# A hybrid encoder on one core: two query tiles loaded ahead of the bias rows, and epsilon of the convolution's layer norm added on VectorE

## The chip, the cores and the metric

The kernel runs on one core of a Trainium2 chip. The time is device time in microseconds (us) of a whole execution; a kernel is timed by the median of several executions. Engines are named as in the profile: PE is TensorE's matmuls, PEld its weight loads, DVE is VectorE, ACT ScalarE, POOL GpSimd, and SP (SyncE) issues the transfers (DMAs).

## The reference

One layer of an encoder runs over two requests with shared weights: a prompt of 512 tokens and a sample of 1024 tokens, model width 1024, everything in float32. Cut to what matters:

```python
h = rmsnorm(x); z = h @ w_in                      # q, k, v, and two conv halves ca, cb
a = window_attn(q, k, v, bias, |i-j| <= 128, sink) # 8 heads, 2 kv heads, blocks of 128 queries
c = dwconv31(ca * sigmoid(cb))                     # 512 channels
c = silu(layernorm(c, g, b))                       # (c - mean) * rsqrt(var + 1e-6) over the channels
x = x + concat(a, c) @ w_out
h = rmsnorm(x); u = dwconv3(h @ w_up)
x = x + (silu(u[:FF]) * u[FF:]) @ w_down           # FF = 2816
y = rmsnorm(x)
```

The attention adds to each score a bias that depends on head and distance alone: for each head one table of 128 x 384 numbers serves all blocks.

## The kernel before

Every float32 product is made of three matmuls: each operand is split into a high and a low part, and high x high, high x low and low x high are accumulated. The projection has the lines L354, L355 and L357 for these three, 128 x 128 weights against 512 columns.

The stages overlap. TensorE first does the prompt's input projection (to about 96 us), then the sample's (to about 345 us), into which the prompt's attention, convolution norms and output projection are woven step by step: they are Python generators (`attention`, `scores`, `values`, `conv_norm`, `out_half`) that are advanced between the projection's matmuls. In the same way the sample's attention is woven into the prompt's feed-forward (to about 600 us); the sample's norms and output projection follow, and then its feed-forward up (from about 740 us) and down (from 1148 us), whose matmuls stand in an order written out by hand. In the earlier part a scheduler of the framework orders each engine's instructions, by the order in which the code issues them and by its own simulated times. On-chip buffers come from a pool of numbered slots (q0..., h0..., s0...): a new tile waits until the last users of its slot are done, so the issue order of the tiles also decides which slot each gets. Names such as h56_198 are slot h56, tile number 198.

The places that matter here:

- *Queries.* `evac` with "q" splits a projected query block and writes it to a scratch buffer in DRAM, qsd, in pieces of 128 KB (L448). `load_q(u)` loads it back for one unit u (one block of 128 queries, one kv head, four heads) as a tile of 128 x 512 numbers, 256 KB (L646). `scores(u)` calls `load_q(u)` and `load_q(u + 1)`, multiplies with the keys (L682, two matmuls of 256 to 384 columns per head), and adds the bias on DVE (L689).
- *Bias.* `load_bias` loads eight rows, one for each head, 192 KB each (L631), from a DRAM table bbd. It is called once, after the prompt's projection, and before any `load_q`.
- *Behind the scores.* ACT takes exponentials (L707), DVE completes the sums and takes a reciprocal (L705, L710, L711), ACT and POOL scale (L715, L717), and TensorE transposes the result (L737) for the product with the values.
- *Convolution.* A depthwise convolution of 31 taps runs mostly as DVE operations (L409); some taps are done by ACT and POOL (L401, L402). A finished channel block is written to DRAM, cvd (L419).
- *The convolution's layer norm.* `conv_norm(i)` runs for each of the 12 blocks of 128 tokens: transposes (L812), mean and variance on DVE (L814, L815), then 1/sqrt(var + eps) on POOL as two operations of one number per partition (`rstd_of`, L214: times 1/n plus eps; L215: to the power -1/2), then the normalisation on DVE (L818), transposes back (L824), scale and shift on ACT (L827), tanh and the product with it (L829 to L832).
- *Splitting weights.* `split` casts a raw weight chunk to its high part on ACT (L237) and subtracts on POOL or DVE (L238). ACT also evacuates finished banks of the projection (L430).
- *The prompt's feed-forward.* Its small convolution of three taps runs on DVE (L977) and ACT (L981).

Of the kernel before, what the change touches and what calls it, by code (L numbers as in the profile page):

```python
# [29 lines left out]
EPS = 1e-6  # L30
# [143 lines left out]
def tile_hybrid_encoder(ctx: ExitStack, tc: tile.TileContext, xs, xsT, rel_bias, norm_attn_g, w_in,  # L174
                        attn_sink, w_out, norm_ffn_g, w_up, w_down, norm_final_g, packed, onehot, outs):
    nc = tc.nc
# [18 lines left out]
    def sm(n):  # L195
        return sb.tile([n])

    def bank(job):
        return banks.tile([NT], among=use[job])
# [13 lines left out]
    def rstd_of(ss, n, out):  # L213
        nc.gpsimd.tensor_scalar(out, ss, 1.0 / n, EPS, op0=ALU.mult, op1=ALU.add)  # L214
        nc.gpsimd.tensor_tensor(out, out, nhalf[:], op=ALU.pow)  # L215

    def power(out):
        nc.gpsimd.tensor_tensor(out, out, nhalf[:], op=ALU.pow)
# [122 lines left out]
    def drain(queue):  # L341
        while queue:
            advance(queue)
# [284 lines left out]
    def load_bias():  # L628
        for h in range(NH):
            bt = sb.tile([3 * P])  # L630
            nc.sync.dma_start(bt[:], bass.AP(b0.tensor, b0.offset + h * NT + P - 1, [[NH * NT - 1, P], [1, 3 * P]]))  # L631
            bias.append(bt)

    load_bias()


    blocks = [(G, b) for G in GR for b in range(G["nb"])]
    NB = len(blocks)
    qt, cats, units, rawcat = {}, {}, {}, {}
# [1 line left out]
    def load_q(u):  # L641
        if u < 2 * NB and u not in qt:
            q = sb.tile([GRP, P], F32R)
            i, kv = divmod(u, 2)
            nt, b = divmod(i, 4)
            nc.sync.dma_start(q[:].bitcast(F32), qsd[nt][b, :, kv * GRP:(kv + 1) * GRP, :])  # L646
            qt[u] = q

    def window(i):
        G, b = blocks[i]  # L650
        return [k for k in (b - 1, b, b + 1) if 0 <= k < G["nb"]]
# [13 lines left out]
    def scores(u):  # L665
        i, kv = divmod(u, 2)
        load_q(u)
        if blocks[min(u + 1, 2 * NB - 1) // 2][0] is blocks[i][0]:
            load_q(u + 1)
# [51 lines left out]
    def cat_of(i, part):  # L721
        if (i, part) not in cats:
            cats[i, part] = (sb.tile([4, P], F32R), sb.tile([4, P], F32R))
        return cats[i, part]
# [45 lines left out]
    def split_cat(i, eng):  # L770
        raw = rawcat.pop(i)
        hi, lo = cats[i, 0] = (sb.tile([4, P], F32R), sb.tile([4, P], F32R))
        flat = lambda t: t[:].rearrange("p j t -> p (j t)")
        nc.scalar.copy(flat(hi), raw[:])
        eng.tensor_tensor(flat(lo), raw[:], flat(hi).bitcast(F32), op=ALU.subtract)
# [16 lines left out]
    def load_conv(i):  # L792
        G, b = blocks[i]
        cv = cvs[i] = sb.tile([4, P])
        nc.sync.dma_start(cv[:], cvd[G["g"]][:, :, b * P:(b + 1) * P])
        if G["g"] == 1 and i not in rawcat:
            load_cat(i)

    def conv_norm(i):
        G, b = blocks[i]  # L800
        if G["g"] == 0:
            drain(convs)
        cat = cat_of(i, 1)
        if i not in cvs:
            load_conv(i)
            yield 0.0
        cv = cvs.pop(i)
        if G["g"] == 1:
            split_cat(i, nc.vector)
        pt = bank("norm")  # L810
        for c in range(4):
            nc.tensor.transpose(pt[:, c * P:(c + 1) * P], cv[:, c, :], ident[:])  # L812
        st, mv, rs = sm(6), sm(2), sm(1)
        nc.vector.bn_stats(st[:], pt[:])  # L814
        nc.vector.bn_aggr(mv[:], st[:])  # L815
        rstd_of(mv[:, 1:2], 1.0, rs[:])
        xh = sb.tile([CCH])
        nc.vector.tensor_scalar(xh[:], pt[:], mv[:, 0:1], rs[:], op0=ALU.subtract, op1=ALU.mult)  # L818
        del pt
        for _ in range(YN if G["g"] == 0 else 3):  # L820
            yield 0.0
        p2 = bank("norm")
        for c in range(4):
            nc.tensor.transpose(p2[:, c * P:(c + 1) * P], xh[:, c * P:(c + 1) * P], ident[:])  # L824
        y, t = sb.tile([4, P]), sb.tile([4, P])
        for c in range(4):
            nc.scalar.activation(y[:, c, :], p2[:, c * P:(c + 1) * P], AF.Identity,  # L827
                                 scale=lng[:, c:c + 1], bias=lnb[:, c:c + 1])
        nc.scalar.activation(t[:], y[:], AF.Tanh)  # L829
        nc.vector.scalar_tensor_tensor(t[:], t[:], 1.0, y[:], op0=ALU.add, op1=ALU.mult)  # L830
        nc.scalar.copy(cat[0][:], t[:])
        nc.vector.tensor_tensor(cat[1][:], t[:], cat[0][:].bitcast(F32), op=ALU.subtract)  # L832
        yield 0.0
# [73 lines left out]
    def prompt():  # L907
        yield from attention(0, 8, {u: conv_norm(u - 4) for u in range(4, 8)})
        kt.clear(), vt.clear(), qt.clear(), bias.clear()
        pace.update(rate=RBO, late=CLO)  # L910
        for n in range(2):
            for kc in range(KC):
                if (kc, n) not in wor:
                    load_wo(kc, n)
            yield 0.0
            for kc in range(KC):
                split_wo(kc, n, kc % 2 < DW)
                if kc % 2 == 1:
                    yield 0.0
            for i in range(4):  # L920
                if n == 0 and i == 3:
                    for kc in range(WOP):
                        load_wo(kc, 1)
                yield from out_half(i, n)
            wo.clear()
        yield from make_h2(0, 0)
# [129 lines left out]
    def sample():  # L1056
        sink_columns()
        yield from attention(8, 24)
        kt.clear(), vt.clear(), qt.clear(), bias.clear(), score_rows.clear()
        use.update(norm="a")  # L1060
        pace.update(rate=RN)
        for m in range(KC + WOA):
            if m in (2, 4):
                load_cat(m // 2 + 3)
            if m < KC:
                load_wo(m, 0)
            if m >= WOA:
                split_wo(m - WOA, 0, True)
                yield 0.0
        drain(late)  # L1070
        for m in range(NE):
            yield from conv_norm(4 + m)
        load_conv(4 + NE)
        for kc in range(KC):
            load_wo(kc, 1)
            yield 0.0
# [174 lines left out]
    def right_halves():  # L1251
        for kc in range(KC):
            split_wo(kc, 1, True)
            yield 0.0

    side.extend((right_halves(), conv_norm(4 + NE)))
    side.extend(pair_sums(p) for p in (*range(SOON), NPAIR - 1))
    pace.update(rate=2.2)
# [607 lines left out]
```

## Time and profile before

| | us |
|---|---|
| three runs | 1490.27, 1491.04, 1492.84 |
| median | 1491.04 |
| profiled execution | 1491.56 |
| its span, first to last instruction | 1489.8 |
| mean granted TensorE clock | 0.998 |
| TensorE's longest wait | 2.90 |

The profile's page gives the busy time of each engine; a list of waits gives, for each engine and line, the time it stood idle and what released it; a timeline gives start and duration of each instruction (or of a run of equal ones, "x4"), with the idle time before it and its releaser in brackets. A windows row gives the length of a stretch, then the busy time of PE, PEld, DVE, ACT and POOL with the number of instructions, the granted clock (1.00 is full), the share of the time that the 16 DMA engines were busy, and GB/s. Matmuls are pipelined: the duration of one (0.39 us) is longer than the distance between two starts.

### The profile page before, as it was taken

The numbers are of one execution on the slowest core, as the hardware profiler recorded it, in microseconds if no ns is written. First come the engines' busy times: TensorE is split into PE (matmuls) and PEld (weight loads), VectorE is DVE, ScalarE is ACT, GpSimd is POOL, SyncE is SP. The second block draws the span as 40 slices with busy tenths as digits, with TensorE's granted clock in tenths as the row PEclk, the third lists the DMA queues.
The fourth block names the chain that finished last, engine by engine and source line by source line (L and its number), as shares of the span: only waits on it lengthen the run. The fifth ranks groups of instructions, "written<-read, shape, count | busy, mean of one in ns | idle before, by whom it ended". The sixth has DMA issues, their size and how long they took to land.

```text
span 1489.8 us, 19831 instructions
## 1 busy us (share of the span) xinstructions
PE 1473.5 (99%) x6808; PEld 1221.1 (82%) x6808; DVE 1136.3 (76%) x1619; ACT 796.9 (53%) x1415; POOL 677.7 (45%) x539
## 2 busy tenths in 40 slices
PE   9999999999999999999999999999999999999998
PEld 7878888887888888878888888888888888888886
DVE  5999988778689875666868777777776945569875
ACT  8556565336777776444465544554445633444254
POOL 6962445235665576763326555555544000003345
PEclk9999999999999999999999999999999999999999
DMA  8963346274433337883213333333332672356644
GB/s 290 294 187 85 93 120 188 86 234 133 132 114 119 121 121 226 268 312 131 82 57 107 106 106 107 106 102 100 103 107 83 225 264 86 110 173 228 217 166 170
DMA packets 222049, 225.60 MB, mean 151 GB/s; under 512 B 12363, under 2 KB 162131, under 8 KB 221820
## 3 DMA queue, kind: packets, MB, share of 16 engines
q1 hardware_dynamic: 221804, 224.08, 47.0%
q8 instruction: 53, 0.87, 0.2%
q14 instruction: 48, 0.39, 0.1%
q10 hardware_dynamic: 144, 0.26, 0.0%
HBM read 165.29 MB, written 60.05 MB: 151 GB/s over the span
## 4 chain that ended last, share of the span: by engine, by line
PE 48%; POOL 3%; DMA 3%; issue 2%; DVE 2%; ACT 1%; SPq 0%; POOLq 0%; DVEq 0%; ACTq 0%
PE w L1237 9%; PE w L1239 9%; PE w L1238 9%; PE w L1589 5%; PE w L1588 5%; PE w L1587 5%; PE u L848 1%; PE u L850 1%; PE u L849 1%; DMA h<-in_w_out 1%; POOL q L1097 1%; PE c L850 1%; PE c L849 1%; PE c L848 1%; DMA c<-in_norm_final_g 0%
## 5 line engine op out<-in xcount | busy, mean ns | idle before, releaser
L238 POOL TENSOR_TENSOR q<-q,q 128x1024 fp32r<-128x1024 f32 x71 | 173.1, 2441 | 126.6 <-ACT q L237 49.4
L1100 POOL TENSOR_TENSOR q<-q,q 128x512 fp32r<-128x512 f32 x101 | 141.9, 1412 | 151.8 <-ACT q L1223 140.8
L1100 DVE TENSOR_TENSOR h<-h,h 128x512 fp32r<-128x512 f32 (+2 forms) x202 | 154.9, 800 | 67.8 <-ACT h L1104 30.2
L1589 PE MATMUL w<-h,h 128*128 128x512 f32 x462 | 179.7, 389 | 0.0
L1587 PE MATMUL w<-h,h 128*128 128x512 f32 x458 | 178.2, 389 | 0.0
L1588 PE MATMUL w<-h,h 128*128 128x512 f32 x458 | 178.2, 389 | 0.0
L1237 PE MATMUL w<-h,q 128*128 128x512 f32 x448 | 174.9, 390 | 1.1 <-ACT w L1320 0.8
L1239 PE MATMUL w<-h,q 128*128 128x512 f32 x448 | 174.3, 389 | 0.0
L1238 PE MATMUL w<-h,q 128*128 128x512 f32 x426 | 165.7, 389 | 0.0
L409 DVE SCALAR_TENSOR_TENSOR c<-c,cvw,c 128x512 f32<-128x512 f32 x209 | 156.8, 750 | 3.0
L354 PE MATMUL u<-h,q 128*128 128x512 f32 x368 | 146.7, 399 | 2.0 <-DVE h L977 2.0
L355 PE MATMUL u<-h,q 128*128 128x512 f32 x368 | 144.4, 392 | 0.0
L357 PE MATMUL u<-h,q 128*128 128x512 f32 x360 | 141.3, 393 | 0.1
L1097 POOL TENSOR_TENSOR q<-q,q 128x1024 f32<-128x1024 f32 x12 | 32.8, 2748 | 230.4 <-DMA h<-gb 190.0
L1104 ACT CAST h<-h 128x512 fp32r<-128x512 f32 x120 | 71.8, 620 | 96.4 <-DVE h L1100 43.9
L354 PE MATMUL b<-h,q 128*128 128x512 f32 x264 | 105.5, 400 | 0.0
L357 PE MATMUL b<-h,q 128*128 128x512 f32 x264 | 104.4, 395 | 0.0
L355 PE MATMUL b<-h,q 128*128 128x512 f32 x264 | 103.9, 394 | 0.0
L1589 PEld LDWEIGHTS w<-h,h 128*128 128x128 f32 x462 | 86.7, 188 | 17.8
L1588 PEld LDWEIGHTS w<-h,h 128*128 128x128 f32 x458 | 86.0, 188 | 18.0
L1587 PEld LDWEIGHTS w<-h,h 128*128 128x128 f32 x458 | 86.0, 188 | 17.8
L1237 PEld LDWEIGHTS w<-h,q 128*128 128x128 f32 x448 | 84.1, 188 | 19.1 <-ACT w L1320 1.3
(447 smaller groups left out, 3620.5 us busy)
## 6 DMA issues: line engine op xcount, KB each, us to landing
q<-in_w_up SPq DMA_DIRECT2D x88, 512.0 KB, 4.4
ga<-q SPq DMA_DIRECT2D x64, 256.0 KB, 2.0
h<-ga SPq DMA_DIRECT2D x57, 256.0 KB, 3.3
q<-in_w_in SPq DMA_DIRECT2D x28, 512.0 KB, 5.3
h<-in_w_down SPq DMA_DIRECT2D x52, 256.0 KB, 3.6
q<-in_x_sample SPq DMA_DIRECT2D x15, 512.0 KB, 7.0
h<-qsd SPq DMA_DIRECT2D x24, 256.0 KB, 2.9
x1d<-q SPq DMA_DIRECT2D x11, 512.0 KB, 4.4
```

Of the source, the lines that this page charges most:

```text
L238: ins = (nc.vector if dve else nc.gpsimd).tensor_tensor(lo[:], raw[:], hi[:].bitcast(F32), op=ALU.subtract)
L354: nc.tensor.matmul(out, whi[:, kc, :], hi[:], start=(kc == 0), stop=False)
L355: nc.tensor.matmul(out, whi[:, kc, :], lo[:], start=False, stop=False)
L357: nc.tensor.matmul(out, wlo[:, kc, :], hi[:], start=False, stop=(kc == KC - 1))
L409: nc.vector.scalar_tensor_tensor(acc[:], src(t), w(t), acc[:], op0=ALU.mult, op1=ALU.add)
L1100: (eng or nc.vector).tensor_tensor(out, a, b, op=ALU.subtract)
L1237: nc.tensor.matmul(out, whi[:, s], hi[:], start=(start and c == 0), stop=False, **go)
L1238: nc.tensor.matmul(out, whi[:, s], lo[:], start=False, stop=False, **go)
L1239: nc.tensor.matmul(out, wlo[:, s], hi[:], start=False, stop=(stop and c == 3), **go)
L1587: nc.tensor.matmul(out, sh[:, c], th[:], start=(p == 0), stop=False)
L1588: nc.tensor.matmul(out, sh[:, c], tl[:], start=False, stop=False)
L1589: nc.tensor.matmul(out, sl[:, c], th[:], start=False, stop=(p == NPAIR - 1))
```

## The change

```diff
@@ -631,9 +631,6 @@
             nc.sync.dma_start(bt[:], bass.AP(b0.tensor, b0.offset + h * NT + P - 1, [[NH * NT - 1, P], [1, 3 * P]]))
             bias.append(bt)
 
-    load_bias()
-
-
     blocks = [(G, b) for G in GR for b in range(G["nb"])]
     NB = len(blocks)
     qt, cats, units, rawcat = {}, {}, {}, {}
@@ -645,6 +642,10 @@
             nt, b = divmod(i, 4)
             nc.sync.dma_start(q[:].bitcast(F32), qsd[nt][b, :, kv * GRP:(kv + 1) * GRP, :])
             qt[u] = q
+
+    load_q(0)
+    load_q(1)
+    load_bias()
 
     def window(i):
         G, b = blocks[i]
@@ -813,7 +814,8 @@
         st, mv, rs = sm(6), sm(2), sm(1)
         nc.vector.bn_stats(st[:], pt[:])
         nc.vector.bn_aggr(mv[:], st[:])
-        rstd_of(mv[:, 1:2], 1.0, rs[:])
+        nc.vector.tensor_scalar_add(rs[:], mv[:, 1:2], EPS)
+        power(rs[:])
         xh = sb.tile([CCH])
         nc.vector.tensor_scalar(xh[:], pt[:], mv[:, 0:1], rs[:], op0=ALU.subtract, op1=ALU.mult)
         del pt
```

The query tiles of units 0 and 1 are now issued in the code ahead of the eight bias rows, and take their slots ahead of them. In the layer norm eps is added by a DVE operation, and POOL does the power alone (`power`, L218). Later lines move by one to three: L646 becomes L643, L682 L683, L707 L708, L715 L716, L737 L738, L818 L820, L830 L832, L832 L834, L977 L979. The scheduler's order changes with it at many places; three of them follow.

SP, the end of the prompt's projection: the last bias rows (bbd) and the first query tiles (qsd), up to the write of a convolution block (cvd). Before:

```order
L631 DMA q6_202_1153<-bbd_406 128x384
L631 DMA h3_200_1148<-bbd_406 128x384
L631 DMA q6_202_1153<-bbd_406 128x384
L631 DMA q3_201_1150<-bbd_406 128x384 x2
L631 DMA q1_203_1156<-bbd_406 128x384
L646 DMA h26_205_1187<-qsd0_163 128x512
L646 DMA h32_206_1189<-qsd0_163 128x512
L231 DMA q10_225_1324<-in_w_in 128x8x128
L646 DMA h11_231_1369<-qsd0_163 128x512
L419 DMA cvd0_169<-h56_125_721 128x512
```

Now:

```order
L631 DMA q6_202_1152<-bbd_406 128x384
L643 DMA h3_200_1148<-qsd0_163 128x512
L631 DMA q6_202_1152<-bbd_406 128x384
L643 DMA q3_201_1150<-qsd0_163 128x512
L631 DMA q1_203_1155<-bbd_406 128x384
L631 DMA h26_205_1161<-bbd_406 128x384
L631 DMA h32_206_1163<-bbd_406 128x384
L643 DMA q3_201_1150<-qsd0_163 128x512
L231 DMA q10_225_1324<-in_w_in 128x8x128
L643 DMA h11_231_1369<-qsd0_163 128x512
L419 DMA cvd0_169<-h56_125_721 128x512
```

Unit 0's tile moved from the sixth bias row's rear (slot h26) to the place of a bias row (slot h3), unit 1's (slot h32 before, q3 now) follows two rows later, and two bias rows went behind. The cvd write kept its place behind the burst. On PE the first scores moved two matmuls forward in the last bank of the projection.

ACT, the same time: the tap of the convolution into slot h56 (L401), the exponentials of unit 0, and the weight cast L237. Before:

```order
L401 ACTIVATE h56_198_1126<-q11_114_671,cvw_308 128x512
L707 ACTIVATE q4_204_1159,s26_208_1192<-q4_204_1159,s25_207_1191 128x256
L707 ACTIVATE h55_209_1200,s26_208_1192<-h55_209_1200,s25_207_1191 128x256
L707 ACTIVATE q13_210_1212,s26_208_1192<-q13_210_1212,s25_207_1191 128x256
L430 ACTIVATE q9_212_1237<-b1_41_1173 128x512
L707 ACTIVATE q13_210_1212,s26_208_1192<-q13_210_1212,s25_207_1191 128x256
L709 ACTIVATE s27_211_1218<-s27_211_1218 128x4
L707 ACTIVATE q9_212_1237,s29_215_1242<-q9_212_1237,s28_214_1241 128x256
L715 ACTIVATE q4_204_1159<-q4_204_1159,s26_208_1192 128x256
```

Now:

```order
L401 ACTIVATE h56_198_1126<-q11_114_671,cvw_308 128x512
L237 CAST q12_244_1456<-q10_225_1324 128x1024
L708 ACTIVATE h55_209_1196,s26_208_1192<-h55_209_1196,s25_207_1191 128x256
L708 ACTIVATE q13_210_1201,s26_208_1192<-q13_210_1201,s25_207_1191 128x256 x2
L430 ACTIVATE q9_211_1217<-b1_41_1177 128x512
L708 ACTIVATE q9_211_1217,s26_208_1192<-q9_211_1217,s25_207_1191 128x256
L710 ACTIVATE s27_212_1219<-s27_212_1219 128x4
L708 ACTIVATE h56_215_1245,s29_214_1241<-h56_215_1245,s28_213_1240 128x256
L708 ACTIVATE h42_216_1250,s29_214_1241<-h42_216_1250,s28_213_1240 128x256
L716 ACTIVATE h55_209_1196<-h55_209_1196,s26_208_1192 128x256
```

The cast, which stood fifteen instructions later, now stands between L401 and the exponentials, and one more exponential of the next unit stands ahead of the scaling.

DVE, near 633 us, where a convolution norm of the sample ends (product with the tanh, then its low part) beside the prompt's feed-forward. Before:

```order
L830 SCALAR_TENSOR_TENSOR h14_1012_6446<-h14_1012_6446,h42_1011_6445 128x512
L977 SCALAR_TENSOR_TENSOR h35_1022_6495<-u0_350_6433,fw_309,h35_1022_6495 128x511
L832 TENSOR_TENSOR h48_1000_6386<-h14_1012_6446,h39_999_6385 128x512
L977 SCALAR_TENSOR_TENSOR h35_1022_6495<-u0_350_6433,fw_309,h35_1022_6495 128x511
L238 TENSOR_TENSOR h35_1046_6628<-h29_1030_6553,h0_1045_6627 128x512
```

Now:

```order
L832 SCALAR_TENSOR_TENSOR h11_1010_6444<-h11_1010_6444,h53_1009_6443 128x512
L834 TENSOR_TENSOR h48_998_6384<-h11_1010_6444,h39_997_6383 128x512
L979 SCALAR_TENSOR_TENSOR h35_1020_6493<-u0_350_6431,fw_309,h35_1020_6493 128x511 x2
L238 TENSOR_TENSOR h35_1044_6626<-h29_1028_6551,h60_1043_6625 128x512
L238 TENSOR_TENSOR h1_1046_6630<-h30_1030_6565,h32_1045_6629 128x512
```

The operation that took the place between the two of the feed-forward (L832, now L834) stands ahead of both.

## The prediction, made before the changed kernel was run

> **What bounds the kernel now.** The page comes first, to see which engine has no time to spare.
>
> ```profile
> span 1489.8 us, 19831 instructions
> PE 1473.5 (99%) x6808; PEld 1221.1 (82%) x6808; DVE 1136.3 (76%) x1619; ACT 796.9 (53%) x1415; POOL 677.7 (45%) x539
> ```
>
> TensorE is busy for all but 16.3 us of its span, and the change neither adds nor removes a matmul. So time can come only from TensorE's gaps, or from matmuls that run slower than usual. The second view is TensorE's list of waits: what it waited for, total, times, longest.
>
> ```profile
> PE u L682 <- DMA h<-qsd: 2.9, 1, 2.9
> PE u L354 <- DVE h L977: 2.0, 2, 1.1
> PE a L824 <- DVE h L818: 1.0, 1, 1.0
> ```
>
> The longest wait of the kernel is the first scores of the prompt (L682), which wait for the load of a query tile from the scratch buffer qsd: the load that the change moves. The third waits for the layer norm that the change edits. Third view: TensorE's timeline around the first wait (start, duration, and in brackets the idle time and its releaser).
>
> ```profile
> 98.11 0.39 PE L354 MATMUL b<-h,q 128*128 128x512 f32 x1
> 98.34 0.39 PE L355 MATMUL b<-h,q 128*128 128x512 f32 x1
> 101.63 0.48 PE L682 MATMUL u<-h,h 128*128 128x256 f32 x2 [2.90 <-DMA h<-qsd]
> ...
> 102.48 0.63 PE L354 MATMUL b<-h,q 128*128 128x512 f32 x1
> 102.90 0.63 PE L355 MATMUL b<-h,q 128*128 128x512 f32 x1
> ...
> 105.46 0.53 PE L357 MATMUL b<-h,q 128*128 128x512 f32 x1
> 105.83 0.39 PE L354 MATMUL b<-h,q 128*128 128x512 f32 x1
> ...
> 106.52 0.39 PE L682 MATMUL u<-h,h 128*128 128x256 f32 x2
> 106.75 0.40 PE L354 MATMUL b<-h,q 128*128 128x512 f32 x1
> ```
>
> Matmuls overlap, so what counts is start to start: 0.23 us for a 512-column one when fed (98.11 to 98.34), 0.42 after the wait (102.48 to 102.90). The wait is therefore paid twice. The windows view, with the granted clock and the DMA share in its last columns, says the same.
>
> ```profile
> 98.60:101.60 3.00, 0.13 (x1) 0.00 (x0) 2.93 (x5) 0.00 (x0) 0.58 (x1) 1.00 0.89 253
> 101.60:105.90 4.30, 4.27 (x16) 3.68 (x17) 3.97 (x12) 0.74 (x2) 0.00 (x0) 0.60 0.65 224
> 105.90:112.00 6.10, 6.10 (x32) 5.17 (x31) 4.88 (x18) 5.56 (x20) 2.23 (x2) 1.00 0.15 43
> ```
>
> **The price of the wait.** L682 could have started at 98.34 + 0.23 = 98.57; it started at 101.63, which is 3.06 us lost. From there to 105.83 TensorE did eight 256-column matmuls and seven 512-column ones. At the rate of 106.52 (two of the small ones in 0.23 us, a large one in 0.23) these take 4 x 0.23 + 7 x 0.23 = 2.53 us; they took 4.20, so 1.67 went to the low clock. Together **4.7 us** hang on this load.
>
> [...]
>
> **The load order, first on SyncE.** The queue's timeline (issue times) is as follows.
>
> ```profile
> 93.25 0.55 SPq L631 DMA_DIRECT2D q<-bbd  x1
> 94.33 0.33 SPq L631 DMA_DIRECT2D h<-bbd  x1
> 94.70 1.85 SPq L631 DMA_DIRECT2D q<-bbd  x4
> 96.59 0.90 SPq L646 DMA_DIRECT2D h<-qsd  x2
> ...
> 98.99 0.32 SPq L419 DMA_DIRECT2D cvd<-h  x1
> ```
>
> And the summary of line 646, all its 24 loads, from issue to landing:
>
> ```profile
> DMA to landing us min/median/max: 2.6/2.9/5.0
> ```
>
> The two query tiles are issued last of this burst, at 96.59, and 96.59 + 5.0 = 101.6 is TensorE's release: this load is the slowest of its 24. In the changed order (the rows in the part on the change) the first tile takes the buffer h3 and the place of the bias row issued at 94.33, and the second follows two places on. By the median its landing is 94.33 + 2.9 = 97.2, by the maximum 99.3. The scheduler also puts the scores two matmuls earlier on TensorE: 98.57 less 2 x 0.23 is 98.11. So 0.9 us to spare by the median, 1.2 us late by the maximum. I take the median, since less stands ahead of it, and count the wait as gone: -4.7. The four bias rows that unit 0 uses stay ahead of or beside it (the fourth is the one issued at 93.25); the last ones pass behind both tiles and are used by unit 1 only, whose scores run 8 us later.
>
> **What is late next: ScalarE.** Its timeline, with DVE, POOL and TensorE at the end of the chain:
>
> ```profile
> 105.16 0.72 ACT L401 ACTIVATE h<-q,cvw 128x512 f32<-128x512 f32 x1 [8.45 <-DMA cvd<-h]
> 105.78 0.49 ACT L707 ACTIVATE q<-q,s 128x256 f32<-128x256 f32 x1
> ...
> 108.23 0.19 ACT L709 ACTIVATE s<-s 128x4 f32<-128x4 f32 x1
> ...
> 109.46 0.51 ACT L715 ACTIVATE q<-q,s 128x256 f32<-128x256 f32 x1 [0.54 <-DVE s L711]
> ...
> 112.95 1.05 ACT L237 CAST q<-q 128x1024 fp32r<-128x1024 f32 x1 [0.61 <-PE b L355]
> 113.91 0.59 ACT L430 ACTIVATE h<-b 128x512 f32<-128x512 f32 x1
> 114.57 0.27 PE L737 MATMUL a<-ident,q 128*128 128x128 f32 x1
> ...
> 115.36 0.48 PE L355 MATMUL b<-h,q 128*128 128x512 f32 x1
> ```
>
> L401, a tap of the convolution, writes into buffer h56, and waits for the write of its previous tenant to DRAM (cvd), issued at 98.99 and landed about 105.1. The exponentials of unit 0 (L707) stand behind it on ScalarE. Today that hides behind TensorE's own stall. In the changed order L401 keeps its place and its buffer, the same bytes stand ahead of the cvd write, so it lands when it did. And behind L401 now stands a weight cast (L237, 112.95 to 113.91: 0.96 us) ahead of the exponentials. So: first exponential 105.78 + 0.96 = 106.7; three of them at 0.5, then the evacuation of bank b1 (L430, 0.58), ending near 108.8; the fourth and L709's counterpart end near 109.4; the reciprocal on DVE and the start of the scaling need the 1.04 us that lie between 108.42 and 109.46, so scaling runs from 110.4 (beside two exponentials of the next unit) to 111.8.
>
> TensorE, 4.7 us earlier, wants bank b1 at 112.98 - 4.7 = 108.2 (seven matmuls of 0.23 before 114.57) and waits 0.6 to 0.7 there; it reaches the eight transposes, which now stand one matmul later, at 114.57 - 4.7 + 0.23 + 0.65 = 110.7. Half of them need the last scaled row, so they end near 112.3 instead of 110.7 + 0.79 = 111.5: 0.8 to 1.2 more, the larger if the cvd write lands a little later than before. Two waits, together **+1.4 to +1.9**, each shorter than the 1.11 us that left TensorE's clock alone at L977. I take 1.6. Net of this part: -4.7 + 1.6 = **-3.1 us**. Bounds: -4.7 if ScalarE isn't held, 0 if it is held until the old end.
>
> **The epsilon on VectorE.** It removes 12 POOL operations of [128x1] and adds as many on DVE, one in each convolution norm.
>
> ```profile
> 653.43 0.17 DVE L815 BATCH_NORM_AGGREGATE s<-s 128x2 f32<-128x6 f32 x1
> ...
> 654.19 0.19 POOL L214 TENSOR_SCALAR s<-s 128x1 f32<-128x1 f32 x1
> 654.46 0.74 POOL L1037 TENSOR_TENSOR c<-c,c 128x256 f32<-128x256 f32 x1
> ...
> 655.15 0.55 POOL L215 TENSOR_TENSOR s<-s,nhalf 128x1 f32<-128x1 f32 x1
> ...
> 655.74 0.81 DVE L818 TENSOR_SCALAR h<-a,s,s 128x512 f32<-128x512 f32 x1 [2.15 <-POOL s L215]
> ...
> 656.70 0.63 PE L824 MATMUL a<-ident,h 128*128 128x128 f32 x4 [1.03 <-DVE h L818]
> ```
>
> Nearest rows for the new DVE operation: L815's 0.17 us as the upper bound, nothing as the lower; 12 x 0.17 = 2.0 us on an engine with 350 us idle, against 12 x 0.27 (654.19 to 654.46) = 3.2 us on POOL. Only at this one norm does TensorE wait for the chain. It gets shorter by 0.27, or by 1.0 if the power no longer queues behind L1037; its transposes, though, stand one matmul (0.23) earlier. The reverse stands 20 us before: at the norm that ends at 635, DVE's L832 now goes ahead of two L977, and TensorE waits for the second.
>
> ```profile
> 634.26 0.74 DVE L977 SCALAR_TENSOR_TENSOR h<-u,fw,h 128x511 f32<-128x511 f32 x1
> 634.37 0.62 ACT L831 CAST h<-h 128x512 fp32r<-128x512 f32 x1 [0.26 <-DVE h L830]
> ...
> 636.99 0.47 PE L354 MATMUL u<-h,q 128*128 128x512 f32 x1 [0.88 <-DVE h L977]
> ```
>
> L832 needs L831, which ends at 634.99, so the L977 that filled 634.26 to 635.0 moves behind it: +0.7. Between -1.0 and +0.7 for both places, I take **0**. The seam near 346 us (L977's wait of 1.11) also gets another order of transposes and VectorE work, bounded by the same size, -1.1 to +0.9; 0 again. Elsewhere DVE waits for TensorE, not the reverse.
>
> **The sum.** The profiled run took 1491.56 us, 1.76 of it outside the span; 1491.56 - 3.1 = 1488.5. The median of the three runs lies 0.52 lower, at 1491.04, so the forecast for the median is **1488.0** (-0.2%).
>
> **The rivals.**
> - *ScalarE doesn't hold TensorE.* If the cvd write lands sooner, nothing takes the wait's place: 1491.0 - 4.7 = 1486.3. For it: the DMA share falls to 0.65 and then 0.15 right behind. Against: the write still stands behind the same bytes. 0.17.
> - *The wait moves whole: no change.* The transposes are forecast to end at 112.3, with one matmul more done than at 115.36 before, so 3.3 us are left. If the cvd write lands 2.5 to 3.3 us later than today's 105.1, ScalarE's chain shifts by as much and the result is 1490.4 to 1491.0; a late first tile leads there only together with that. For it: three loads that stood behind the tiles now stand between or ahead of other traffic, at a DMA share of 0.89. Against: the bytes ahead of the write are the same. Chance 0.24. [...] With the tile landing at 99.3 alone, TensorE would wait 1.2 us there, less at ScalarE, and the time would stay near 1488.
> - *Slower: the new wait throttles.* If the cvd write lands 4.4 us late (109.5), the transposes end at 116.7, 1.1 us later than before with its extra matmul (115.6); and TensorE then stands at b1 for over the 2.90 us that slowed it before, and pays the low clock's 1.67 again: +2.8, that is 1493.8. It decides from a landing 3.3 us later than today. The DMA share speaks for some delay, the equal bytes against so much. 0.13.
> - *The change doesn't do what it says*, the tile being held by its buffer h3 until after 96.6: that buffer was free at 94.33 for the bias row. Time as before, 1491.0. 0.05.
>
> **How the numbers follow.** Forecast 0.41, between 1487.0 and 1489.3 by the bounds of ScalarE's part and of the seams. A measurement here can tell about 0.2% from no change, that is 1488.06, so the forecast is split: 0.24 below, 0.17 above. Faster: 0.24 + 0.17 = 0.41; same: 0.17 + 0.24 + 0.05 = 0.46, less 0.05 for the upward bounds of the seams at 346 and 635; slower: 0.13 + 0.05 = 0.18. For 8 in 10 the range takes in the whole gain with a seam's gain (1485.8) and stops short of the throttled case, at 1492.5.
>
> **What would show it.** Right: no wait of L683 (today's L682) on qsd, granted clock 1.00 from 98 to 108, two waits of TensorE near 108 and 111 us on ScalarE, each about 1 us, the transposes done by 112.3, and the stretch behind 116 us shifted by 3 us as a block. Wrong: a wait for qsd above 1 us; a clock below 0.9 near 110; a cvd write that lands after 107; or a new wait of over 1 us beyond 320 us, which would eat the shift.

## The result and the profile after

| | before | after |
|---|---|---|
| median of 7 runs each, us | 1491.23 | 1496.24 |
| lowest to highest | 1488.48 to 1493.50 | 1494.34 to 1498.80 |
| profiled execution | 1491.56 | 1498.80 |
| ratio to before, 95% interval | | 1.0034 [1.0021, 1.0046] |

The change makes the kernel about 5 us slower; 1488.0 was forecast, and 1496.24 lies above the forecast's range. The profiled execution is the slowest of its seven, 7.2 us above the profile of before, so the shares below add up to 7.2, not to 5.

The page of after: span, busy time of each engine. The work is the same, and DVE's instructions are up by twelve as POOL's are down by twelve.

```profile
span 1497.0 us, 19822 instructions
PE 1475.9 (99%) x6808; PEld 1222.3 (82%) x6808; DVE 1135.4 (76%) x1631; ACT 797.0 (53%) x1415; POOL 672.6 (45%) x527
```

TensorE's list of waits in after (total, times, longest): the same two names as in before, qsd and the layer norm, and new ones between them.

```profile
PE a L683 <- DMA h<-qsd: 2.5, 1, 2.5
PE b L354 <- ACT q L430: 2.3, 1, 2.3
...
PE a L826 <- DVE h L820: 1.6, 1, 1.6
...
PE u L752 <- ACT h L740: 1.2, 1, 1.2
PE u L350 <- ACT q L237: 1.1, 1, 1.1
```

A list has no times of day. The wait for qsd is not the old one: TensorE's timeline of after has the prompt's first scores (98.54) without a wait, and a wait on ScalarE 13 us behind them.

```profile
98.54 0.48 PE L683 MATMUL u<-h,h 128*128 128x256 f32 x2
...
111.27 0.50 PE L354 MATMUL b<-h,q 128*128 128x512 f32 x1 [2.35 <-ACT q L430]
...
113.86 0.33 PE L738 MATMUL a<-ident,h 128*128 128x128 f32 x1 [0.47 <-ACT h L716]
```

So the step that the change aims at happened: 98.54 instead of 101.63, and no low clock (1.00 granted from 98 to 107). Matched matmul by matmul, TensorE of after was 4.2 us ahead of before near 107 us, and only 0.5 us ahead near 120. It then fell behind: by 1.1 us at 157 (L752 waits 1.19 us for ScalarE's L740), by 1.9 from 260 to 326 (the transposes of the fourth convolution block wait 0.63 us at 258.73 for its load), by 9 near 348, by 7.4 from 356 to 610, by 7.2 at the end. Two places hold most of the loss: **108 to 115 us**, where 3.7 of the 4.2 us go back, and **326 to 356 us**, the seam where the sample's attention begins, which costs 5.5. The windows there, of before (columns as in the prediction; the granted clock stands third from the end):

```profile
335.00:340.00 5.00, 5.00 (x27) 3.88 (x25) 4.11 (x6) 2.31 (x3) 3.51 (x2) 1.00 1.06 321
340.00:345.00 5.00, 4.95 (x22) 4.05 (x22) 2.32 (x5) 3.50 (x4) 3.31 (x3) 1.00 0.75 236
```

And of after:

```profile
335.00:340.00 5.00, 1.98 (x15) 1.30 (x13) 4.63 (x8) 3.46 (x5) 3.41 (x3) 0.88 1.08 345
340.00:345.00 5.00, 5.00 (x14) 4.13 (x15) 4.79 (x7) 0.66 (x1) 2.12 (x1) 0.50 1.09 306
```

TensorE's timeline of after says what it waits for there:

```profile
334.23 0.50 PE L350 MATMUL u<-h,q 128*128 128x512 f32 x1 [1.07 <-ACT q L237]
...
336.73 0.66 PE L308 MATMUL a<-ident,q 128*128 128x128 f32 x4 [0.47 <-DVE h L311]
...
339.93 0.77 PE L683 MATMUL a<-q,h 128*128 128x256 f32 x2 [2.54 <-DMA h<-qsd]
340.49 0.63 PE L354 MATMUL u<-h,q 128*128 128x512 f32 x1
340.92 0.63 PE L355 MATMUL u<-h,q 128*128 128x512 f32 x1
341.35 0.63 PE L683 MATMUL a<-q,h 128*128 128x256 f32 x2
341.77 7.20 PE L350 MATMUL u<-h,q 128*128 128x512 f32 x23
```

Three waits make 4.08 us, the last for the *sample's* first query tile. The granted clock is 0.50 there as well: from 340.49 to 348.81 TensorE did 26 matmuls' worth (25 large ones and two half ones), which at 0.23 each take 6.0 us and took 8.3, so 2.3 more. Against these 6.4 us stands a wait of 1.11 us that before has at 346. The wait that was removed at 98 us has come back at 340, in the same form and with a similar penalty.

Why the sample's tile is late is seen on SP's timeline (issue times): the load of the prompt's fourth convolution block (cvd), the first write of the prompt's output projection (x1d), and the sample's first query tiles (qsd). In before:

```profile
230.26 0.57 SPq L795 DMA_DIRECT2D q<-cvd  x1
...
296.82 0.33 SPq L856 DMA_DIRECT2D x1d<-q  x1
...
326.97 1.35 SPq L646 DMA_DIRECT2D h<-qsd  x2
```

In after:

```profile
255.54 0.56 SPq L796 DMA_DIRECT2D h<-cvd  x1
...
304.36 0.33 SPq L858 DMA_DIRECT2D x1d<-q  x1
...
335.03 1.35 SPq L643 DMA_DIRECT2D h<-qsd  x2
```

The fourth block's tile got another slot. In before it took half of a q slot, and the load was issued without a wait; in after it took an h slot, the load stands 25 us later, and SP still waits 1.5 us there for L834 on DVE, the end of an earlier block's norm. The fourth block's norm needs that tile, and in the code the output projection stands behind that norm: all but its first two matmuls run from 274.2 us on in after, from 265.3 in before. Its first write waits on SP for DVE (L855, the sum with the residual) and came 7.5 us later. From 277.5 us until that write, at 304.36, SP issued nothing, and the sample's loads behind it came 8 us later as well. That the early tiles take their slots first is all that links this to the change.

### The profile page after: what moved, and what is told of

Its sections match the earlier page's. It is cut to its first block, busy times and chain, and to the rows that moved or that the text cites. A ratio compares the mean times of both kernels' runs of the same rounds, so it can differ in the third digit from the quotient of the medians.

```text
span 1497.0 us, 19822 instructions
## 1 busy us (share of the span) xinstructions
PE 1475.9 (99%) x6808; PEld 1222.3 (82%) x6808; DVE 1135.4 (76%) x1631; ACT 797.0 (53%) x1415; POOL 672.6 (45%) x527
## 4 chain that ended last, share of the span: by engine, by line
PE 48%; POOL 3%; issue 2%; DMA 2%; DVE 2%; ACT 1%; SPq 0%; POOLq 0%; DVEq 0%; ACTq 0%
PE w L1239 9%; PE w L1240 9%; PE w L1241 9%; PE w L1589 5%; PE w L1591 5%; PE w L1590 5%; PE u L851 1%; PE u L852 1%; PE u L850 1%; DMA c<-gt 1%; POOL q L1099 1%; PE c L852 1%; PE c L850 1%; PE c L851 1%; POOL s L218 0%
## 5 line engine op out<-in xcount | busy, mean ns | idle before, releaser
L354 PE MATMUL u<-h,q 128*128 128x512 f32 x368 | 146.8, 399 | 0.0
L354 PE MATMUL b<-h,q 128*128 128x512 f32 x264 | 104.9, 397 | 2.3 <-ACT q L430 2.3
L237 ACT CAST q<-q 128x1024 fp32r<-128x1024 f32 (+1 forms) x72 | 74.7, 1044 | 48.8 <-DMA q<-in_w_in 19.0
```

The lines of the kernel that those rows point to most:

```text
L354: nc.tensor.matmul(out, whi[:, kc, :], hi[:], start=(kc == 0), stop=False)
```

## The experiments

In the expectations the theories have letters and are spelled out where they are first used. The one that matters most, C, says that the seam's loss comes from the slots: taking h3 and q3 early moves all later tiles to other slots, the fourth convolution block's among them. D, in e9 to e11, is C with ScalarE's wait for the cvd write as a loss of its own. All ratios are to the kernel before on the same chip, with 95% intervals. Places ("at 116") are where TensorE's matched matmuls stand against the profile of before.

| run | what it has | median, us | ratio |
|---|---|---|---|
| e1 | early tiles, old norm | 1494.27 | 1.0024 [1.0010, 1.0038] |
| e2 | epsilon on DVE alone | 1492.80 | 1.0013 [1.0004, 1.0023] |
| e3 | early tiles, old slots, old norm | 1489.65 | 0.9992 [0.9983, 1.0001] |
| e4 | changed kernel, sample's tiles early too | 1496.43 | 1.0036 [1.0024, 1.0049] |
| e5 | changed kernel, fourth block from a q slot | 1497.03 | 1.0045 [1.0033, 1.0057] |
| e6 | e3 with epsilon on DVE | 1490.63 | 0.9997 [0.9986, 1.0008] |
| e7 | e3 with a spare buffer for L401 | 1486.45 | 0.9977 [0.9967, 0.9987] |
| e8 | epsilon on DVE in the sample's norms alone | 1491.08 | 1.0001 [0.9990, 1.0012] |
| e9 | new slots, old load order, old norm | 1493.69 | 1.0009 [0.9997, 1.0021] |
| e10 | before with the spare buffer | 1494.05 | 1.0017 [1.0006, 1.0028] |
| e11 | changed kernel with the spare buffer | 1494.14 | 1.0018 [1.0007, 1.0028] |
| e12 | epsilon on DVE in the prompt's norms alone | 1491.21 | 0.9998 [0.9987, 1.0009] |
| e13 | e7, fourth block from a late h slot | 1486.52 | 0.9977 [0.9966, 0.9987] |
| e14 | e7 with epsilon on DVE | 1488.86 | 0.9987 [0.9974, 1.0000] |

### e1 and e2: each part alone

e1 is the change without its last hunk, e2 the last hunk alone.

> Only the load order is changed, the norm is as before. Theory A (the load order gives other slots to later tiles, SP's queue stands in another order near 304 to 335 us, and the seam between the two projections loses 4.6 us): slower than before by 3 to 6 us, 1494 to 1497, with waits of TensorE near 334 to 340 us for a query tile and a raw weight chunk, and its first scores no longer waiting for qsd near 98 us. Theory B (the epsilon on VectorE costs it, in the norms' chains): no slower than before, 1487 to 1492.

> Only the norm is changed, the loads are as before. Theory A: within 1.5 us of before (1490 to 1492.5), TensorE's wait of 2.9 us near 98 us still there and the seam near 346 us as before. Theory B: slower by 3 to 6 us.

The load order alone makes the kernel slower, so the loss is not epsilon's. e1 is ahead by 4.2 us at 107, by 2.2 at 116, by 0.5 at 157 and by nothing from 272 to 326, and the seam costs 4.2 (a clock of 0.56 in 335 to 340). Epsilon alone costs a little: +0.13%, with an interval just off zero. In e2's profile the loss stands at the seam, where a wait of 2.03 us on DVE, 1.11 in before, was followed by matmuls 0.42 us apart (347.51 to 347.93) instead of 0.23.

### e3 and e6: the early load with the old slots

```diff
     def load_bias():
         for h in range(NH):
-            bt = sb.tile([3 * P])
-            nc.sync.dma_start(bt[:], bass.AP(b0.tensor, b0.offset + h * NT + P - 1, [[NH * NT - 1, P], [1, 3 * P]]))
-            bias.append(bt)
+            bias.append(sb.tile([3 * P]))
+    def bias_rows():
+        for h in range(NH):
+            nc.sync.dma_start(bias[h][:], bass.AP(b0.tensor, b0.offset + h * NT + P - 1, [[NH * NT - 1, P], [1, 3 * P]]))
...
             load_q(u + 1)
+        if u == 0:
+            bias_rows()
```

The tiles are taken in the old order (bias first), the loads issued in the new one. For the sample nothing changes: there `load_bias` is called a second time (the part on the places has it called once), and `bias_rows()` follows it directly. e6 adds the last hunk of the change.

> The norm as before; buffers are taken in the old order, only the transfers of five bias rows are issued behind the first two query tiles. Theory A: slots, and with them the order near 304 to 350 us, stay as before, so the early gain is left without the later loss: the wait near 98 us is gone or below 1 us, the cvd write lands near 105 since no further query tile stands ahead of it, and the time is 1486.5 to 1490, 1 to 4.5 us below before. Rival (an earlier query tile gains nothing, since ScalarE's wait for the cvd write near 105 us ends the stretch in any case): 1490.5 to 1492.

> Both edits, but with all buffers taken in the old order (as in the third run), the epsilon on VectorE. Theory C: the norms near 612 to 660 us give back about 1 us, no loss at the seam: 1487.5 to 1490.5. Rival (the epsilon itself costs about 2 us, as its run alone had it): 1491 to 1493.

With the old slots the same early load loses nothing at the seam: 4.8 us ahead at 107, 2.2 at 116, and 1.8 to 2.2 from there until 610. e3 and e1 differ by 4.6 us in median. What still goes back, 2.6 us at 108 to 115, is ScalarE's wait for the cvd write, which stays in e3; its ACT timeline:

```profile
106.85 0.72 ACT L401 ACTIVATE h<-q,cvw 128x512 f32<-128x512 f32 x1 [10.22 <-DMA cvd<-h]
```

### e7, e10 and e11: ScalarE's wait taken away

```diff
                     pr = sb.tile([NT])
+                    if g == 0 and c == 2 and k == noff - 1:
+                        pr = odd.tile([P, NT], F32, tag="d0", name="d0_spare", bufs=1)
                     nc.scalar.activation(pr[:], src(t), AF.Identity, scale=w(t))
```

The tap that waits for h56 (L401) writes to a buffer that has long been free; h56 stays reserved, so no other slot moves. e7 puts this into e3, e10 into before, e11 into the changed kernel.

> The third run, and the one tap of the convolution that stood on ScalarE behind the cvd write now writes into a buffer that has been free for long (the slot stays reserved, so all others keep theirs). Theory C: no wait for cvd on ScalarE, TensorE's waits near 109 and 112 us (1.2 and 0.5 us) go, TensorE is 4 to 4.5 us ahead of before at 120 us; what of it is left at the end is 2 to 4.5 us, 1486.5 to 1489. Rival (VectorE, busy for 95% of 120 to 200 us, takes the lead back): TensorE loses it again before 260 us, and the time is that of the third run, 1489 to 1490.5.

> Before, with the one tap on ScalarE writing into the free buffer. Theory D: TensorE waits for the query tile till about 101.6 us as before, and ScalarE's wait stood in its shadow: 1490 to 1492, a gain below 1.5 us. Rival (ScalarE's wait for the cvd write was what limited before as well): 1486 to 1489, as in the seventh run.

> The changed kernel, with the one tap on ScalarE writing into the free buffer. Theory D: the lead of 4 us at 107 us is kept at 120 us, and the later losses stay (the fourth convolution block's slot, the seam): 1492 to 1494.5. Rival (the slots matter only because ScalarE was held at 107 us): 1486 to 1489.

e7 beats both kernels: 1486.45, -0.23%. Its ACT timeline shows bank b1's evacuation (L432, the old L430) and the first scaling (L721) where TensorE no longer waits for them:

```profile
104.99 0.58 ACT L432 ACTIVATE q<-b 128x512 f32<-128x512 f32 x1
...
107.47 0.51 ACT L721 ACTIVATE q<-q,s 128x256 f32<-128x256 f32 x1 [0.21 <-DVE s L717]
```

The lead is 4.5 us at 107 and at 124, and 4.6 at 610: the 4.7 us that the prediction priced, kept nearly whole. e11 keeps 4.4 to 4.6 until 245 and 4.0 until 326, and loses 4.2 at the seam, for the sample's query tile (2.48 us) and a clock of 0.71 (335 to 340). So the two losses are separate, and each remedy removes its own.

e10 fell out of both theories, which had it at 1490 to 1492 and at 1486 to 1489; it is slower. Without the early load the spare buffer changes SP's order around the burst. The wait on TensorE's timeline of e10:

```profile
103.59 0.77 PE L684 MATMUL u<-h,h 128*128 128x256 f32 x2 [4.28 <-DMA h<-qsd]
```

And the issue of the three query tiles on its SP timeline:

```profile
98.13 1.41 SPq L648 DMA_DIRECT2D h<-qsd  x3
```

The query tiles are issued at 98.13 (96.59 in before) and the wait grows from 2.90 to 4.28. That accounts for 1.7 us of the profile's 3.2; another 1.2 go at the seam, where a wait on DVE is 2.23 us instead of 1.11. Why the scheduler puts them later was not followed up.

### e4, e5, e9 and e13: the seam

e4 starts from the changed kernel and edits the place where the sample's bias rows are loaded:

```diff
+    load_q(8)
+    load_q(9)
     load_bias()
```

e5 starts from the changed kernel and edits `load_conv`:

```diff
-        cv = cvs[i] = sb.tile([4, P])
+        cv = cvs[i] = sb.tile([4, P], among="q" if i == 3 else None)
```

e13 starts from e7 and edits the same line (`halved` lets a tile take half of a q slot):

```diff
+        halved = sb.halved
+        if i == 3:
+            sb.halved = None
-        cv = cvs[i] = sb.tile([4, P])
+        cv = cvs[i] = sb.tile([4, P], among="h" if i == 3 else None)
+        sb.halved = halved
```

e9 starts from before, takes the slots in the changed order and issues the two query tiles behind the bias rows, where `scores(0)` used to load them:

```diff
             q = sb.tile([GRP, P], F32R)
...
             qt[u] = q
+            if u > 1:
+                fill_q(u)
...
+    load_q(0)
+    load_q(1)
+    load_bias()
...
+        if u == 0:
+            fill_q(0)
+            fill_q(1)
```

`fill_q(u)` holds the old transfer of `load_q`.

> The changed kernel, with the sample's first two query tiles also loaded ahead of its bias rows. If the six bias rows ahead of that tile are what TensorE waits for at 340 us, the wait of 2.5 us and the low clock behind it (about 1.8 us) go: 1491 to 1493. If the whole SP queue is late there (weights, keys and values too), another load takes its place and the time stays at 1495 or above.

> The changed kernel, with one tile elsewhere: the load of the prompt's fourth convolution block takes a slot of the q kind, as before the change, and no longer h10, which a DVE operation of the third block's norm frees late. Theory C (the new slot makes that load 25 us late, so the fourth norm and the output projection start 11 us late, and SP's queue brings the sample's tiles late to the seam): the output projection starts before 256 us again, TensorE's waits at 334 to 340 us and the low clock there go, and the time falls by 3 to 6 us from the changed kernel's 1496.2, to 1490 to 1493. Rival (the seam is lost through the early order of loads itself, or through the epsilon): no change, 1495 or above.

> The norm as before, all tiles take the slots that the changed order gives them, but the first two query tiles are issued behind the bias rows again. Theory D (the loss comes from the slots that later tiles get, not from the order of the transfers near 95 us): slower than before by 3 to 6 us, 1494 to 1497.5, with the first scores waiting for qsd and the fourth convolution block and the output projection late as in the changed kernel. Rival (the early order of transfers causes it): 1490 to 1492.

> The kernel of e7 (early query tiles, old slots, spare buffer, old norm; -0.23%), with one thing made worse on purpose: the load of the prompt's fourth convolution block takes a slot of the h kind that comes free late, as it does in the changed kernel, and stands nine rows further back on SP, behind loads of w_out. Theory C (the late fourth block holds SP's queue and with it the prompt's output projection and the sample's first scores): the load is issued 10 us or more later than in e7, TensorE's waits at the seam near 326 to 346 us grow and a low clock follows; 3 to 5 us lost there, 1489.5 to 1492. Rival (it is no single tile, but the whole shuffle of slots): the seam loses under 1 us and the time stays at that of e7, 1486 to 1488.

*e4*: the wait for the sample's query tile goes, and others take its place (0.66 us for a bias row, 0.55 for a weight cast). The median stays at that of after. That the burst as a whole is late, and not its order the cause, fits this; the run alone doesn't show it.

*e5*, its SP timeline:

```profile
245.01 0.58 SPq L796 DMA_DIRECT2D q<-cvd  x1
...
329.85 1.32 SPq L643 DMA_DIRECT2D h<-qsd  x2
```

And two waits of its TensorE timeline:

```profile
266.69 0.50 PE L851 MATMUL u<-h,h 128*128 128x512 f32 x1 [1.89 <-DVE h L238]
...
350.07 0.47 PE L354 MATMUL u<-h,q 128*128 128x512 f32 x1 [2.21 <-DVE h L979]
```

The fourth block is loaded 10 us earlier than in after, the sample's query tiles 5 us earlier, and the seam costs 1.1 us instead of 5.5. So the mechanism holds at the seam. Its forecast of the time does not: about as much is lost at a split of w_out (266.69, 2.2 us with what follows) and at a norm near 660 (a wait of 2.66 us). That the other slot moved these too is likely, and not shown.

*e9*: the load is late here too (252.67, query tiles at 329.58), with the transfers near 95 us in their old order: the slots alone make it late. The seam costs 2.1 us: three waits of 1.2, 0.7 and 0.6 us, at full clock (1.00 from 335 to 350). Its ratio is within the error of no change, and its median 2.2 us above that of before; theory D had put it slightly higher, from 1494. The profile is the fastest of the twelve runs, 2.8 us below their median, so the seam may cost more in the others. In the profiles, the late load is worth about 2 us at full clock, and 4.2 (e1) to 5.5 (after) where a low clock came with the waits (0.56 in 335 to 340, and 0.50 in 340 to 345).

*e13*, its SP timeline:

```profile
240.12 0.56 SPq L805 DMA_DIRECT2D h<-cvd  x1
...
322.63 1.28 SPq L650 DMA_DIRECT2D h<-qsd  x2
```

The load comes 14.5 us later than in e7 (225.63) and costs nothing; the query tiles of the sample are issued as in e7 (322.91). That went against the theory as stated. Put on TensorE's own schedule (e13 runs 4.7 us ahead of before at that time, e5 0.2 behind), a load at 245 is early enough in both; in e1, e4, e9, e11 and after it comes at about 254 to 255, and all five have the late seam. The point from which it matters lies in between; it was not closed in further.

### e8, e12 and e14: epsilon

e8 puts epsilon on DVE in the eight norms of the sample alone, e12 (with 1 for 0 in the first line added) in the four of the prompt:

```diff
-        rstd_of(mv[:, 1:2], 1.0, rs[:])
+        if G["g"] == 0:
+            rstd_of(mv[:, 1:2], 1.0, rs[:])
+        else:
+            nc.vector.tensor_scalar_add(rs[:], mv[:, 1:2], EPS)
+            power(rs[:])
```

e14 is e7 with the last hunk of the change.

> Before, with the epsilon on VectorE in the sample's eight norms only: all that comes ahead of about 600 us keeps its order. If the epsilon's loss lies in the prompt's part (the order near 200 to 350 us) this is no slower than before: 1488.5 to 1491, with about 1 to 1.5 us gained near 612 to 660 us. If it costs in the sample's norms or behind them: 1491.5 to 1493.

> Before, with the epsilon on VectorE in the prompt's four norms only. If the 1.9 us that the epsilon cost alone come from the prompt's part (the wait near 346 us, which crossed into the low clock there): 1492 to 1494. If they were of the sample's norms, or the draw of its runs: 1490 to 1491.8.

> The kernel of e7 with epsilon added on VectorE in all twelve norms. It differs from e11 (changed kernel with the spare buffer, +0.18%) only in the slots that the early tiles and bias rows take and in the place of the last bias rows. Theory C (the slots): the whole gain of e7 is kept, 1485.5 to 1488, ratio 0.996 to 0.9985. Rival (epsilon, in a schedule that is no longer held at the query tile, costs what separates e11 from e7): 1491 to 1494, ratio 1.000 to 1.002.

e14 and e11 differ only in the slots and in the place of the last bias rows: 0.9987 [0.9974, 1.0000] against 1.0018 [1.0007, 1.0028]. The intervals don't touch: some 5 us of e11's time belong to the slots (or those rows), not to epsilon. Against e7 epsilon costs 2.4 us in median, with intervals that overlap. The norm near 653 in e14 shows what can be lost. DVE's timeline, where epsilon is added and the normalisation follows:

```profile
647.78 0.15 DVE L822 TENSOR_SCALAR s<-s 128x1 f32<-128x1 f32 x1
652.22 0.81 DVE L825 TENSOR_SCALAR h<-a,s,s 128x512 f32<-128x512 f32 x1 [4.28 <-POOL s L218]
```

And POOL's:

```profile
648.76 0.74 POOL L1038 TENSOR_TENSOR c<-c 128x256 f32<-128x256 f32 x1 [3.23 <-DMA c<-gt]
...
650.95 0.72 POOL L1044 TENSOR_TENSOR c<-c,c 128x256 f32<-128x256 f32 x1
651.63 0.55 POOL L218 TENSOR_TENSOR s<-s,nhalf 128x1 f32<-128x1 f32 x1
```

Epsilon is added by 647.93. The power (L218) could run then, on an idle POOL; it stands behind four operations of which the first waits for a load (c<-gt) until 648.76, and runs at 651.63. TensorE waits 2.85 us for this norm, 0.44 in e7.

## Why the prediction was wrong, point by point

The forecast was a gain of 3.1 us net. In the profile 4.2 us were gained and 11.6 lost: 3.7 behind ScalarE, 1.6 at 149 us, 0.8 at 259 and 5.5 at the seam. Two of the signs of being wrong that it names came true, a cvd write landing after 107 and a new wait of over 1 us beyond 320.

- **The wait at 98 us: right.** No wait of L683 there, clock 1.00, 4.2 us of lead at 107.
- **Its price, 4.7 us: right.** e7 keeps 4.5 to 4.6 us until 610, and its median is 4.9 below that of before.
- **ScalarE is what is late next: right in its mechanism, wrong in size.** The two waits that were forecast (on L430 and L716) are in after, 2.35 and 0.47 us, and the cast (108.23) stands ahead of the exponentials as the order said. The term was +1.6; it measured 3.7 in after, 2.6 in e3. The step that failed: "the same bytes stand ahead of the cvd write, so it lands when it did". After's ACT timeline:

```profile
107.60 0.72 ACT L401 ACTIVATE h<-q,cvw 128x512 f32<-128x512 f32 x1 [10.62 <-DMA cvd<-h]
108.23 1.03 ACT L237 CAST q<-q 128x1024 fp32r<-128x1024 f32 x1
109.16 0.50 ACT L708 ACTIVATE h<-h,s 128x256 f32<-128x256 f32 x1
```

After's SP timeline:

```profile
95.00 0.33 SPq L643 DMA_DIRECT2D h<-qsd  x1
...
95.91 0.37 SPq L643 DMA_DIRECT2D q<-qsd  x1
...
97.74 0.43 SPq L643 DMA_DIRECT2D q<-qsd  x1
98.22 0.44 SPq L231 DMA_DIRECT2D q<-in_w_in  x1
98.75 0.53 SPq L643 DMA_DIRECT2D h<-qsd  x1
99.66 0.36 SPq L419 DMA_DIRECT2D cvd<-h  x1
```

Four query tiles stand ahead of the write, not three; the rows of the change show it, and the prediction read past it. The write was issued 0.67 us later and landed near 107.6, not 105.1. That is 2.5 us, just where the rival "the wait moves whole" begins, and up to 120 us after behaves as that rival says. The fourth tile is not shown as the cause: e3 has three tiles ahead, issues the write at 99.13, and it lands near 106.85. So with three tiles ahead the time from issue to landing was 6.1 us in before and 7.7 in e3, and with four 7.9 in after; why stays open.
- **A term that it doesn't have: L752 at 149 us.** TensorE waits 1.19 us for ScalarE's L740, which costs 1.6. Waits of 0.6 to 1.25 us stand there in e1, e4, e5 and e9 too, and none in e11 or in a kernel with the old slots; it was not followed up.
- **The seam near 346, "0 again", bounded by -1.1 to +0.9: wrong, and the largest error.** It cost 5.5 us. This is the step that failed most: the bound was taken from the wait that stood there, as if only the order of a few instructions could change. What changed were the slots, and 80 us ahead of the seam: the fourth block's load, the output projection, the sample's loads, and at the end a wait with its low clock. e3 against e1, and e14 against e11, show the slots as the cause; e9 shows that they alone make the fourth block late, and e5 that the late block carries the loss to the seam. e13 shows the limit: late by 14.5 us it cost nothing.
- **Epsilon, 0 between -1.0 and +0.7: about right.** With all twelve on DVE: +0.13% (e2), and, by difference of ratios, +0.05% (e6 to e3), +0.10% (after to e1), +0.10% (e14 to e7); with eight (e8) or four (e12) nothing. Only e2's interval excludes zero, and the four with all twelve lie on the side of a cost, of 1 to 2 us; near zero it came out by terms that were both wrong. At 635 nothing was lost (the wait of 0.88 us on L977 went), and the norm behind it got no shorter (TensorE waits 1.60 us there in after, 1.03 before), since the power still queues behind POOL's operations, as in e14 (in after epsilon is added by 659.68, and the power runs at 661.54).
- **The slower rival** (a new wait at b1 that throttles) named the right form at the wrong place. The 2.35 us there brought no low clock (1.00 from 110 to 115), and the 2.54 us at 340 came with one (0.50 from 340 to 345). It went by the length of a wait; the last part has waits of much the same length with a low clock behind them and without.

## What to carry to other kernels

A buffer taken earlier moves every later tile that shares the pool: compare the slots, not only the instruction order, up to the end of the program, and look at each load that its new slot puts later. Where a wait is removed, take the next one in the chain away with it: here the early load with its new slots (+0.24%) and the spare buffer alone (+0.17%) made the kernel slower, and both together, on the old slots, made it 0.23% faster. Before a small operation moves to another engine, look at what follows it on the old one: in e14 epsilon was ready at 647.93, and the power, queued behind four operations of POOL, ran at 651.63.

## What the runs showed of the hardware

**Waits of much the same length came with a low clock and without.** Seven waits of TensorE with what followed: the distance of two starts of 512-column matmuls right behind the wait, from the timelines, and the granted clock of a stretch around or behind its end, where a windows row gives it.

| run | wait, us | ends at, us | start to start behind it, us | granted clock |
|---|---|---|---|---|
| before | 1.11 (L354) | 346.53 | 0.24 (346.84 to 347.08) | 1.00 in 346 to 350 |
| e2 | 2.03 (L354) | 347.20 | 0.42 (347.51 to 347.93) | |
| e5 | 2.21 (L354) | 350.07 | 0.24 (350.38 to 350.62) | |
| after | 2.35 (L354) | 111.27 | 0.23 (111.61 to 111.84) | 1.00 in 110 to 115 |
| after | 2.54 (L683) | 339.93 | 0.43 (340.49 to 340.92) | 0.50 in 340 to 345 |
| before | 2.90 (L682) | 101.63 | 0.42 (102.48 to 102.90) | 0.60 in 101.6 to 105.9 |
| e10 | 4.28 (L684) | 103.59 | 0.42 (104.58 to 105.00) | |

The 2.03 us in e2 had slow matmuls behind them, the longer 2.21 in e5 and 2.35 in after had not. So in these runs the length of a wait alone didn't tell whether it would be paid twice, and what else it takes they do not show.

**Equal code scatters by more than the question.** The unchanged kernel ran between 1487.73 and 1496.65 us in one set of 35 runs. The profiles of before and after lie 7.2 us apart, the medians 5.0. Single profiles therefore show where time goes, and only the ratios show how much.
